# Both ends, the S5 tables and the start of attention of a hybrid S5 and attention block

## The chip, the cores and the metric

One core of a Trainium2 chip runs the whole block in one launch. The metric is the device time of one execution in microseconds (us). Each engine takes its own instructions in order: PE does matmuls, DVE, ACT and POOL work on tiles, SP issues most DMAs; ACT issues some from its own queue. Semaphores tie the queues together.

## The reference, cut to what matters

```python
h    = modulate(rmsnorm(x, norm1_g), sh1, sc1)            # x 1024x1024, one sequence; mod = silu(c) @ w_ada + b_ada
u, q, k, v, gate_a, gate_b = split(h @ w_in, ...)         # 512, 512, 512, 512, 1024, 1024 columns
# S5: 32 groups of 16 channels, 64 complex states; a linear recurrence over time
y    = gelu(Re(states @ C) + d_skip * u)
y    = y * sigmoid(y @ w_glu + b_glu)
y_a  = y @ w_a
# stick-breaking attention, 8 heads of 64, strictly causal, blocks of 128 queries
y_b  = stick_breaking_attention(q, k, v) @ w_b
x    = x + g1 * ((sigmoid(gate_a) * y_a + sigmoid(gate_b) * y_b) @ w_o)
h    = modulate(rmsnorm(x, norm2_g), sh2, sc2)
x    = x + g2 * ((silu(h @ w_ffn_gate) * (h @ w_ffn_up)) @ w_ffn_down)    # hidden width 2816
return rmsnorm(x, norm_f_g)
```

All is float32. A float32 product is made from three matmuls of rounded parts: each operand is split into a high part (a cast to fp32r) and a low part (the difference), and `PRODUCTS` runs high x high, high x low, low x high.

## The kernel before

The stages run one after the other, and PE's order is the order of the stages, with the matmuls of other stages put between where a scheduler finds room.

**Start (0 to 60 us).** x comes in tiles of 128 rows. ACT and DVE make sums of squares, PE transposes the tiles (L643, into `tp`), and the adaLN vectors are made meanwhile: `ada_products` (L989) multiplies `cond` with 512-column pieces of `w_ada`, which arrive as `pb`, and L621 sums over partitions into `adap`. L649 to L654 modulate, L660 projects u.

**S5 (90 to 265 us).** Four steps m of eight groups. DVE builds tables (`o`, L279 to L281, and `rt`, L291 to L296; DMAs L301 lay `rt` into `tz`, which POOL's memset L298 clears first), runs the scan (L327 to L342) and writes the states `h` (L345). PE adds `u x tz` (L354) and `h x o` (L355) in `s5a`, ACT copies that to `y` (L357), DMAs write it to `yD`. `o` and `tz` have one buffer each. In the same time PE runs the v projection (`v_proj`, L781) and the gates (`gate`, L760). Their results leave PSUM in turn on ACT and DVE: `vst` (L785), `gst` (L796 DVE, L798 ACT).

**GLU and y_a (254 to 359 us).** `glu` reads `yD` back (L1050) in eight pieces `raw`, L1051 does the gelu and writes with a stride of eight elements, `split` (L1038 ACT cast, L1039 DVE subtraction) makes `yp`, and L760 multiplies into `ga`. `branch_a` multiplies by the gate (L1087, into `na`).

**Attention (359 to 660 us).** `attention` goes through units (head pair, query block, key blocks). PE makes scores `z` (L834), DVE adds the causal mask where the block is on the diagonal (L896), ACT and DVE make log terms (L899 to L904), PE sums them with triangular ones (`acc<-wh,upto`), carried from unit to unit in `row` tiles, and multiplies by V. Between the parts of units `fillers` gives PE matmuls of the later q, k and gate projections (`JOBS`, in numbers `FILL`). The mask and the triangle `upto` are made at its start (POOL L822 to L830, DVE L825), and the carries are cleared there by DVE (L950).

**y_b and on (660 to 1456 us).** `branch_b` begins with the products of `w_b`; between its second and third column `ada_cols` turns the second half of the adaLN vectors into columns (L1030, single-column matmuls). Then come w_o, the FFN, and the last norm. Of the last row tile the sum of squares is taken in two halves (L1464), POOL makes small terms of the first (L1467) and multiplies its left half by `gf` (L1468); `rstd_p` (L510 to L514, ACT and POOL) makes the factor, L1439 and L1440 apply it, two DMAs write.

Of the kernel before, what the change touches and what calls it, by code (L numbers as in the profile page):

```python
# [28 lines left out]
class S5:  # L29
# [233 lines left out]
    def outputs(self, m):  # L263
# [5 lines left out]
        o = work.tile([128, 8, 9, 16], F32, name="o")  # L269
# [27 lines left out]
        tz = work.tile([128, 8, 128], F32, name="tz")  # L297
# [6 lines left out]
    def run(self, m, u_src, y_dst, more):  # L304
# [44 lines left out]
        for hf in range(2):  # L349
# [7 lines left out]
            nc.scalar.copy(y[:, 4 * hf:4 * hf + 4].rearrange("p g c -> p (g c)"), p)  # L357
# [21 lines left out]
FILL = (8, 8, 12)  # L379
JOBS = (("q", 1), ("k", 1), ("g", 0), ("g", 1), ("q", 2), ("k", 2), ("g", 2), ("q", 3), ("k", 3), ("g", 3), ("g", 4), ("g", 5), ("g", 6), ("g", 7))  # L380
# [49 lines left out]
class Block:  # L430
# [132 lines left out]
    def start(self, const, up, s5p):  # L563
# [8 lines left out]
        with self.pool("s0", 1, side="right") as sp, self.pool("s0a", 1, side="right") as ap, self.pool("s5t", 1, side="right") as st, \  # L572
# [66 lines left out]

            def turn(h, k):  # L640
                q = turned[h, k] = tp.tile([P, 512], F32, name="tp")
                for t in range(4):
                    nc.tensor.transpose(q[:, P * t:P * t + P], x[4 * h + t][:, P * k:P * k + P], self.ident)  # L643
# [23 lines left out]
            self.rows(const)  # L667
# [102 lines left out]
    def v_proj(self, vp):  # L770
# [3 lines left out]
        for c in range(2):  # L774
            ws = [self.w3(self.weight(src[:, 4 * a:4 * a + 4, 1536 + 256 * c:1792 + 256 * c], first=self.last_ada), 256) for a in range(2)]
            for t in range(KT):
# [8 lines left out]
                (nc.vector.tensor_copy if t % 2 else nc.scalar.copy)(v, ps[:, 0:256])  # L785
                nc.sync.dma_start(out=self.vD[P * t:P * t + P, 256 * c:256 * c + 256], in_=v)

    def gate(self, g, m, gp, first=None, ring=None, mm=None):
        nc = self.nc
        w = self.w3(self.weight(self.in_cols(2048 + 1024 * g + P * m), first=first, ring=ring, hi_eng=g and nc.gpsimd or None, lo_eng=g and nc.gpsimd or None))  # L790
        for h in range(2):
# [3 lines left out]
            if h:  # L795
                nc.vector.tensor_copy(st, ps)  # L796
            else:
                nc.scalar.copy(st, ps)  # L798
# [37 lines left out]
    def fillers(self, qk, qp, kp, gp):  # L836

        nc = self.nc
# [4 lines left out]
        def load(j):  # L843
            n, i = jobs[j]
            c0 = {"q": 512, "k": 1024, "g": 3072}[n] + P * i
            loaded.append(self.w3(self.weight(self.in_cols(c0), lo_eng=nc.gpsimd, hi_eng=nc.gpsimd if n == "g" else None, ring=rings[j % 3])))
# [28 lines left out]
    def scores(self, u, qk, work):  # L875
# [3 lines left out]
        q, k = qk[u.hp]  # L879
        u.a, s = (work.tile([P, 2, 512], F32, name=t, bufs=b) for t, b in (("wa", WAB2), ("ws", WSB)))  # L880
        u.parts = [work.tile([P, 2, 512], F32R, name=t, bufs=WHB) for t in ("wh", "wl")]
# [12 lines left out]
        if diag:  # L894
            m = P * (2 - len(u.kbs))
            nc.vector.tensor_tensor(a, z, self.mask[:, m:m + f].unsqueeze(1).broadcast_to([P, 2, f]), ALU.add)  # L896
# [45 lines left out]
    def attention(self, qk, qp, kp, vp, op, gp, work):  # L942
# [5 lines left out]
        for n in range(RWB):  # L948
            t = work.tile([P, 2, 512], F32R, name=f"row{n}")
            nc.vector.tensor_scalar(t.rearrange("p a (b c) -> p (a b) c", c=P), self.ident.unsqueeze(1).broadcast_to([P, 8, P]), 0.0, None, ALU.mult)  # L950
# [7 lines left out]
        fill = self.fillers(qk, qp, kp, gp)  # L958
# [6 lines left out]
        for i in range(-LOOK, len(units) + 1):  # L965
# [56 lines left out]
    def ada_cols(self, const, tp, pp):  # L1022

        nc = self.nc
        ps = pp.tile([P, 512], F32, name="pa")
        for a in range(2):
            t = tp.tile([P, 1024], F32, name="ac")
            nc.sync.dma_start(out=t.rearrange("p (a b) -> p a b", a=2), in_=self.aD[:, 2 + 2 * a:4 + 2 * a])
            for k in range(KT):
                nc.tensor.matmul(ps[:, 8 * a + k:8 * a + k + 1], lhsT=t[:, P * k:P * k + P], rhs=self.ones[:, 0:1], start=True, stop=True)  # L1030
# [577 lines left out]
```

## Time and profile before

| | us |
|---|---|
| three runs | 1449.16, 1455.71, 1457.14 (median 1455.71) |
| profiled execution, its time | 1457.32 |
| its span | 1455.6 |
| PE busy | 1408.4 (97%) |
| DVE, ACT, POOL busy | 1076.4, 640.4, 514.1 |
| mean granted TensorE clock | 0.986 |

PE is busy in all but 47.2 us of the span, so what counts is where PE waits, and where its clock is not granted in full. A view by windows shows both. An engine's busy time elsewhere matters only where PE waits for it. The ends of matmuls are modelled.

### The profile page before, as it was taken

How to read it: one execution, taken by the hardware profiler on the slowest of the kernel's cores; microseconds unless marked ns; L12 is line 12 of the kernel's file. 1: busy time of each engine (PE TensorE's matmuls, PEld its weight loads, DVE VectorE, ACT ScalarE, POOL GpSimd, SP SyncE). 2: the span in 40 equal slices, each digit the busy share in tenths (PEclk: the TensorE clock that was granted, in tenths of full speed). 3: DMA queues.
4: the chain of work that ended last, by engine and by line, in shares of the span. 5: the costliest groups of instructions: out<-in, count | busy, mean ns of one | idle time of the engine just before them, and what ended most of it. 6: DMA issues, size and time to landing. Idle time of an engine off the chain costs nothing. (4 is left out here: it accounts for less than half of the span.)

```text
span 1455.6 us, 18298 instructions
## 1 busy us (share of the span) xinstructions
PE 1408.4 (97%) x6730; PEld 1116.9 (77%) x6730; DVE 1076.4 (74%) x1395; ACT 640.4 (44%) x846; POOL 514.1 (35%) x291
## 2 busy tenths in 40 slices
PE   5999998999899999999999999999999999999997
PEld 3799887787666666658888888788888888788886
DVE  4779995456787889887723688777666667899896
ACT  3532112722586867674417543232323333433334
POOL 1010000102111022103400015876767566699394
PEclk9999999999999999999999999999999999999999
DMA  9665655489111112117452223644434369899722
GB/s 339 166 148 164 185 133 139 131 272 330 34 44 46 35 52 73 37 58 238 133 186 88 87 87 112 221 145 155 136 126 146 119 206 373 289 378 359 247 83 116
DMA packets 193561, 233.39 MB, mean 160 GB/s; under 512 B 29500, under 2 KB 128896, under 8 KB 193472
## 3 DMA queue, kind: packets, MB, share of 16 engines
q1 hardware_dynamic: 184336, 224.70, 47.1%
q10 hardware_dynamic: 8912, 7.48, 1.8%
q8 instruction: 53, 0.87, 0.2%
q14 instruction: 36, 0.29, 0.1%
q0 software_dynamic: 224, 0.05, 0.0%
HBM read 162.85 MB, written 68.16 MB: 159 GB/s over the span
## 5 line engine op out<-in xcount | busy, mean ns | idle before, releaser
L475 POOL TENSOR_TENSOR ws<-wb 128x1024 f32<-128x1024 f32 x24 | 60.7, 2527 | 175.8 <-DVE wl L478 148.1
L459 POOL TENSOR_TENSOR wl<-ws,wh 128x1024 fp32r<-128x1024 f32 x12 | 30.8, 2564 | 160.6 <-ACT wh L456 160.1
L927 DVE TENSOR_TENSOR wa<-wa,acc 128x512 f32<-128x512 f32 (+1 forms) x80 | 47.0, 628 | 32.9 <-ACT row L925 30.5
L1349 POOL TENSOR_TENSOR pa<-pa 128x512 f32<-128x512 f32 x30 | 63.4, 2143 | 0.3
L1293 POOL TENSOR_TENSOR f<-f,f 128x512 f32<-128x512 f32 x30 | 53.1, 1797 | 26.1 <-DVE f L1287 20.8
L899 ACT ACTIVATE ws<-wa 128x1024 f32<-128x1024 f32 (+1 forms) x40 | 39.1, 977 | 50.9 <-DVE wa L896 50.4
L904 DVE TENSOR_TENSOR wl<-ws,wh 128x1024 fp32r<-128x1024 f32 (+1 forms) x40 | 57.1, 1427 | 1.0
L478 DVE TENSOR_TENSOR wl<-ws,wh 128x1024 fp32r<-128x1024 f32 x23 | 41.4, 1798 | 20.2 <-ACT wh L477 20.1
L1004 DVE SCALAR_TENSOR_TENSOR acc<-aw,cond,acc 128x512 f32<-128x512 f32 x56 | 45.7, 816 | 10.2 <-DMA aw<-in_w_ada_dram 9.4
L456 ACT CAST wh<-ws 128x1024 fp32r<-128x1024 f32 x24 | 25.2, 1050 | 55.5 <-PE wo L1139 25.7
L902 DVE SCALAR_TENSOR_TENSOR ws<-wa,ws 128x1024 f32<-128x1024 f32 (+1 forms) x40 | 45.5, 1137 | 4.6 <-ACT ws L901 3.6
L834 PE MATMUL z<-q,k 64*128 64x512 f32 (+3 forms) x192 | 42.6, 534 | 6.1 <-DVE wa L896 4.9
L1378 POOL TENSOR_TENSOR pa<-pa,row 128x1024 f32<-128x1024 f32 x14 | 42.5, 3052 | 14.7 <-DMA pa<-in_w_ffn_down_dram 14.7
L1286 ACT ACTIVATE f<-f 128x1024 f32<-128x1024 f32 x20 | 21.2, 1061 | 59.5 <-DVE f L1324 30.8
L930 ACT ACTIVATE wa<-wa 128x1024 f32<-128x1024 f32 (+1 forms) x40 | 38.8, 971 | 19.3 <-DVE wa L927 18.3
L477 ACT CAST wh<-ws 128x1024 fp32r<-128x1024 f32 x23 | 24.1, 1054 | 50.9 <-PE wo L1302 15.6
L458 POOL TENSOR_SCALAR wh<-ws 128x1024 fp32r<-128x1024 f32 x6 | 7.5, 1245 | 105.0 <-issue 36.1
L477 ACT CAST wh<-wb 128x1024 fp32r<-128x1024 f32 x25 | 26.2, 1052 | 39.9 <-PE mm L1423 9.7
L475 POOL TENSOR_TENSOR wgs<-wb 128x1024 f32<-128x1024 f32 x12 | 28.9, 2405 | 40.8 <-DVE wl L478 19.9
L1423 PE MATMUL tq<-f,f 128*128 128x512 f32 x136 | 41.7, 389 | 0.0
L834 PE MATMUL mm<-wa,V 128*64 128x512 f32 (+3 forms) x192 | 39.8, 507 | 0.0
L478 DVE TENSOR_TENSOR wl<-wb,wh 128x1024 fp32r<-128x1024 f32 x25 | 38.1, 1528 | 1.9 <-ACT wh L477 1.9
(862 smaller groups left out, 4693.9 us busy)
## 6 DMA issues: line engine op xcount, KB each, us to landing
wb<-hD SPq DMA_DIRECT2D x40, 512.0 KB, 5.3
aw<-in_w_ada_dram SPq DMA_DIRECT2D x64, 256.0 KB, 4.3
hD<-f SPq DMA_DIRECT2D x30, 512.0 KB, 5.0
ws<-in_w_in_dram SPq DMA_DIRECT2D x23, 512.0 KB, 4.4
wb<-in_w_ffn_gate_dram SPq DMA_DIRECT2D x44, 256.0 KB, 4.2
wb<-in_w_ffn_up_dram SPq DMA_DIRECT2D x44, 256.0 KB, 4.6
ws<-hD SPq DMA_DIRECT2D x20, 512.0 KB, 4.8
x<-in_x_dram SPq DMA_DIRECT2D x16, 512.0 KB, 6.9
```

The source lines that it names most:

```text
L475: (add or nc.gpsimd).tensor_tensor(st, a, b, op)
L477: nc.scalar.copy(h, a)
L478: self.last_lo = (lo or nc.vector).tensor_tensor(l, a, h.bitcast(F32), ALU.subtract)
L834: return self.tc.keep_in_program_order(self.nc.tensor.matmul(*args, **kw))
L902: nc.vector.scalar_tensor_tensor(st, a, 0.0, st, ALU.max, ALU.add)
L904: nc.vector.tensor_tensor(lt, st, ht.bitcast(F32), ALU.subtract)
L927: nc.vector.tensor_tensor(a[:, x, 0:f], a[:, x, 0:f], r[:, x, 0:f], ALU.subtract)
L1004: nc.vector.scalar_tensor_tensor(acc, w[:, j], cj, acc, ALU.mult, ALU.add)
L1293: self.last_sum = nc.gpsimd.tensor_tensor(o, a, b, op)
L1349: self.after(nc.gpsimd.tensor_tensor(t[:, n], part(a), part(b), SIGN_B[i]), first)
L1378: self.after(nc.gpsimd.tensor_tensor(w, w, g2, ALU.mult), first)
L1423: nc.tensor.matmul(ps, lhsT=o[x][:, P * t:P * t + P], rhs=o[y][:, R], start=(j == 0), stop=(j == 3 * np_ - 1))
```

## The change

Five parts. (1) S5's tables `o` and `tz` get two buffers; the gelu is done by the copy of `s5a` out of PSUM (L357), so that `glu` loads y whole in four DMAs and reads it by stride in `split` and in the product with the sigmoid. (2) All `vst` copies are on ACT; the `gst` copies are on ACT, but for the gates that have `first` set, whose copies are all on DVE. (3) At the start PE transposes the identity 78 times before x is there, and 4 and 9 times round the first adaLN products. (4) The mask and triangles are made before `qk_proj`; `gt` and `na` have a pool of their own, with the result that attention's score tiles lie elsewhere; the carries are cleared after the first mask addition; `ada_cols` becomes four jobs "a" among the fillers; six fillers go into each of the last three units. (5) Of the last row tile, DVE instead of POOL multiplies by `gf`, and ACT makes the two small terms.

```diff
-        o = work.tile([128, 8, 9, 16], F32, name="o")
+        o = work.tile([128, 8, 9, 16], F32, name="o", bufs=2)
-        tz = work.tile([128, 8, 128], F32, name="tz")
+        tz = work.tile([128, 8, 128], F32, name="tz", bufs=2)
-            nc.scalar.copy(y[:, 4 * hf:4 * hf + 4].rearrange("p g c -> p (g c)"), p)
+            nc.scalar.activation(y[:, 4 * hf:4 * hf + 4].rearrange("p g c -> p (g c)"), p, AF.Gelu_apprx_tanh)
...
-FILL = (8, 8, 12)
-JOBS = (... ("g", 4), ("g", 5), ("g", 6), ("g", 7))
+FILL = (8, 8, 12, 6)
+JOBS = (... ("g", 4), ("a", 0), ("g", 5), ("a", 1), ("g", 6), ("a", 2), ("g", 7), ("a", 3))
...
+            def idle(n):
+                for _ in range(n):
+                    nc.tensor.transpose(acc[3][:, 0:P], self.ident, self.ident)
...
+            idle(78)
             for t in range(4):
                 square(t, t % 2 == 0)
...
+            idle(4)
             ada_sums(0)
+            idle(9)
...
-                (nc.vector.tensor_copy if t % 2 else nc.scalar.copy)(v, ps[:, 0:256])
+                nc.scalar.copy(v, ps[:, 0:256])
...
-            if h:
-                nc.vector.tensor_copy(st, ps)
-            else:
-                nc.scalar.copy(st, ps)
+            (nc.vector.tensor_copy if first else nc.scalar.copy)(st, ps)
...
+            if n == "a":
+                ps = self.mm.tile([P, 512], F32, name="mm")
+                for k in range(4):
+                    self.pinned(ps[:, k:k + 1], lhsT=loaded[j][:, P * k:P * k + P], rhs=self.ones[:, 0:1], start=True, stop=True)
+                    if k == 3:
+                        s = slice(4 * i, 4 * i + 4)
+                        nc.vector.tensor_tensor(self.mod2[:, s], ps[:, 0:4], self.cols[:, 88 + 4 * i:92 + 4 * i], ALU.add)
+                        ...
+                    yield
+                continue
...
-            t = work.tile([P, 2, 512], F32R, name=f"row{n}")
-            nc.vector.tensor_scalar(t.rearrange("p a (b c) -> p (a b) c", c=P), self.ident..., 0.0, None, ALU.mult)
+            t = rowp.tile([P, 2, 512], F32R, name=f"row{n}")
...
+                if i == -LOOK:
+                    for t in carries:
+                        self.after(nc.vector.tensor_scalar(t..., self.ident..., 0.0, None, ALU.mult), self.masked)
                 some(FILL[1] if i >= 0 else FILL[2])
+            elif i < len(units):
+                some(FILL[3])
...
-            yv = y[:, m].rearrange("p (c j) -> p j c", j=8)
-            for j in (0, 4):
-                raw = yp_.tile([P, 4, P], F32, name="raw", bufs=2)
-                nc.sync.dma_start(out=raw, in_=self.yD[P * m:P * m + P, j:j + 4])
-                nc.scalar.activation(yv[:, j:j + 4], raw, AF.Gelu_apprx_tanh)
+            nc.sync.dma_start(out=y[:, m].rearrange("p (j c) -> p j c", j=8), in_=self.yD[P * m:P * m + P])
         for m in range(4):
-            self.split(yp[:, 0, m], yp[:, 1, m], y[:, m])
+            self.split(*(yp[:, n, m].rearrange("p (c j) -> p c j", j=8) for n in range(2)), y[:, m].rearrange("p (j c) -> p c j", j=8))
...
-                    nc.vector.tensor_tensor(sg, y[:, m, s], sg, ALU.mult)
+                    yv, sv = y[:, m].rearrange("p (j c) -> p c j", j=8), sg.rearrange("p (c j) -> p c j", j=8)
+                    nc.vector.tensor_tensor(sv, yv[:, 64 * h:64 * h + 64], sv, ALU.mult)
...
-            if c == 2:
-                self.ada_cols(const, tp, pa)
...
             if t == ROWS[-1]:
+                nc.vector.tensor_tensor(row[:, L], row[:, L], gf[:, L], ALU.mult)
                 r = self.rstd_p(ss[:, 1:2], small[:, t, 2:3], small[:, t, 3:4], (small[:, t, 4:5], small[:, t, 5:6]))
...
-                            nc.gpsimd.tensor_scalar(small[:, t, n:n + 1], ss[:, 0:1], f / 1024.0, self.eps[:, n - 4:n - 3], ALU.mult, ALU.add)
-                        nc.gpsimd.tensor_tensor(row[:, cs], row[:, cs], gf[:, cs], ALU.mult)
+                            nc.scalar.activation(small[:, t, n:n + 1], ss[:, 0:1], AF.Identity, bias=self.eps[:, n - 4:n - 3], scale=f / 1024.0)
...
+                        self.triangles(s3.enter_context(self.pool("tri", 1)))
                         qk = [self.qk_proj(0, qp, kp, None)]
```

The rest of the diff moves tiles between pools (`rows`, `na`, `row`, `part`, `cp`), widens `eps` and lets `branch_b` begin at another PSUM bank.

How the rows stand on the engines, at three places. The line numbers of the changed kernel are its own: its L767 is L760 of before, L1030 is L1004, L1095 is L1087, L918 is L896, L1004 is L950.

PE at the last step of S5, before: the gate matmuls (`mx<-pa` or `pb` and a weight half) that stand ahead of the last y matmuls (`s5a`).

```order
L760 MATMUL mx<-pb,wl 128x512
L760 MATMUL mx<-pb,wh 128x512 x2
L760 MATMUL mx<-pb,wl 128x512
L354 MATMUL s5a<-u,tz 128x128
L355 MATMUL s5a<-h,o 128x128
```

The same place in the changed kernel:

```order
L767 MATMUL mx<-pa,wl 128x512
L767 MATMUL mx<-pa,wh 128x512 x2
L767 MATMUL mx<-pa,wl 128x512
L354 MATMUL s5a<-u,tz 128x128
L355 MATMUL s5a<-h,o 128x128
```

The last y matmuls have moved up before the second part (`pb`) of that gate; counted over the whole row, 30 gate matmuls that stood ahead of them stand behind them.

DVE at the last states `h` of S5, before (`scr`, `tc`, `tn` are the scan and its rotations; `gst` is a gate's copy):

```order
L345 TENSOR_TENSOR h<-scr 64x4x127 x2
L341 TENSOR_TENSOR scr<-scr,tc 128x4x127
L342 TENSOR_TENSOR scr<-scr,tn 128x4x127
L796 COPY gst<-mx 128x512
L345 TENSOR_TENSOR h<-scr 64x4x127 x2
L459 TENSOR_TENSOR wgl<-wgs,wgh 128x1024
```

And in the changed kernel:

```order
L345 TENSOR_TENSOR h<-scr 64x4x127 x2
L341 TENSOR_TENSOR scr<-scr,tc 128x4x127
L342 TENSOR_TENSOR scr<-scr,tn 128x4x127
L345 TENSOR_TENSOR h<-scr 64x4x127 x2
L459 TENSOR_TENSOR wgl<-wgs,wgh 128x1024
```

One of six `gst` copies (and all eight `vst` copies) that stood ahead of the last `h` is gone there; nothing else is added or taken away ahead of it.

DVE where attention begins, before (`na` is the product with the gate, `acc<-aw,cond,acc` an adaLN sum of a later stage, `row` the carries, `wa<-z,mask` the first masked scores):

```order
L1087 TENSOR_TENSOR na<-ga,gt 128x512
L1004 SCALAR_TENSOR_TENSOR acc<-aw,cond,acc 128x512
L950 TENSOR_SCALAR row_3531<-ident 128x1024
L950 TENSOR_SCALAR row_3533<-ident 128x1024
L825 CAST upto<-tri 128x128
L896 TENSOR_TENSOR wa<-z,mask 128x2x384 x2
```

And in the changed kernel:

```order
L1095 TENSOR_TENSOR na<-ga,gt 128x512 x2
L1030 SCALAR_TENSOR_TENSOR acc<-aw,cond,acc 128x512 x2
L918 TENSOR_TENSOR wa<-z,mask 128x2x384
L1004 TENSOR_SCALAR row_3617<-ident 128x1024
L1004 TENSOR_SCALAR row_3618<-ident 128x1024
L924 SCALAR_TENSOR_TENSOR ws<-wa,ws 128x2x384
L918 TENSOR_TENSOR wa<-z,mask 128x2x384
```

The first mask addition now stands ahead of the carries, the triangle's cast is gone from here (it stands some thirty rows earlier), and one adaLN sum more stands between the last `na` and the mask.

More of the change, by code (lines that the diff above doesn't have):

```diff
@@ L665, in store @@
                 nc.sync.dma_start(out=self.uD[P * m:P * m + P, :, 64 * h:64 * h + 64], in_=u)
-            self.rows(const)
+            self.rows(ap)
             load(0)
@@ L843, in load @@
         def load(j):
+            nonlocal turn
             n, i = jobs[j]
+            if n == "a":
+                t = cp.tile([P, 512], F32, name="ac", bufs=2)
+                nc.sync.dma_start(out=t, in_=self.aD[:, 2 + i])
+                loaded.append(t)
+                return
             c0 = {"q": 512, "k": 1024, "g": 3072}[n] + P * i
-            loaded.append(self.w3(self.weight(self.in_cols(c0), lo_eng=nc.gpsimd, hi_eng=nc.gpsimd if n == "g" else None, ring=rings[j % 3])))
+            loaded.append(self.w3(self.weight(self.in_cols(c0), lo_eng=nc.gpsimd, hi_eng=nc.gpsimd if n == "g" else None, ring=rings[turn % 3])))
+            turn += 1
         for j in range(AHEAD):
@@ L873, in fillers, with scores @@
                         yield
-    def scores(self, u, qk, work):
+    def scores(self, u, qk, part, work):
         nc = self.nc
         q, k = qk[u.hp]
+        u.parts = [part.tile([P, 2, 512], F32R, name=t) for t in ("wh", "wl")]
         u.a, s = (work.tile([P, 2, 512], F32, name=t, bufs=b) for t, b in (("wa", WAB2), ("ws", WSB)))
-        u.parts = [work.tile([P, 2, 512], F32R, name=t, bufs=WHB) for t in ("wh", "wl")]
         z = self.zp.tile([P, 2, 512], F32, name="z")
@@ L940, in values, with attention @@
             self.nc.scalar.copy(out[:, 512 * u.Q:512 * u.Q + 512], g.av)
-    def attention(self, qk, qp, kp, vp, op, gp, work):
+    def attention(self, qk, qp, kp, vp, op, gp, rowp, part, work, cp):
         nc = self.nc
@@ L957, in attention @@
                     units.append(Bag(hp=hp, Q=Q, kbs=kbs, group=g))
-        fill = self.fillers(qk, qp, kp, gp)
+        fill = self.fillers(qk, qp, kp, gp, cp)
         def some(n):
@@ L979, in attention @@
             if i + LOOK < len(units):
-                self.scores(units[i + LOOK], qk, work)
+                self.scores(units[i + LOOK], qk, part, work)
+                if i == -LOOK:
+                    for t in carries:
+                        self.after(nc.vector.tensor_scalar(t.rearrange("p a (b c) -> p (a b) c", c=P), self.ident.unsqueeze(1).broadcast_to([P, 8, P]), 0.0, None, ALU.mult), self.masked)
                 some(FILL[1] if i >= 0 else FILL[2])
+            elif i < len(units):
+                some(FILL[3])
         some(10000)
@@ L1020, in ada_row @@
             nc.vector.tensor_tensor(row[:, js], ps, row[:, js], ALU.add)
[L1022 to L1030, printed above, removed]
-        self.mod2 = const.tile([P, 16], F32, name="mod2")
-        self.G2 = const.tile([P, KT], F32, name="G2")
-        nc.vector.tensor_tensor(self.mod2, ps[:, 0:16], self.cols[:, 88:104], ALU.add)
-        nc.vector.scalar_tensor_tensor(self.G2, self.mod2[:, 8:16], 1.0, self.cols[:, 56:64], ALU.add, ALU.mult)
     def split(self, hi, lo, src, eng=None):
@@ L1144, in attend_out @@
         mod, G = self.mod2, self.G2
-        self.eps = const.tile([P, 19], F32, name="eps")
+        self.eps = const.tile([P, 27], F32, name="eps")
         for n, x in enumerate((1e-6, -0.5e-6, 1.5)):
@@ L1537, in run @@
                     op = s3.enter_context(self.pool("o", 4))
-                    with self.pool("tri", 1) as tri, self.pool("work", 1) as work, self.pool("zp", ZPB, PSUM) as self.zp, self.pool("acc", 1, PSUM) as self.accp, \
+                    with self.pool("row", 1) as rowp, self.pool("part", WHB) as part, self.pool("work", 1) as work, self.pool("zp", ZPB, PSUM) as self.zp, self.pool("acc", 1, PSUM) as self.accp, \
                             self.pool("mx", MXB, PSUM) as mx:
                         self.avp = mg_
-                        self.triangles(tri)
                         self.mm = Turns((mm, "mm"), *[(mx, "mx")] * MXB)
                         qk = [list(qk[0])] + [[None, None] for _ in range(3)]
-                        ops = self.attention(qk, qp, kp, vp, op, gp, work)
+                        with self.pool("cp", 1, side="right") as cp:
+                            ops = self.attention(qk, qp, kp, vp, op, gp, rowp, part, work, cp)
                         spare = []
```

25 lines of the change are left out of this document (15 added, 10 removed).

## Prediction

> **What bounds the kernel now.** I read the page first, then PE's waits, then the windows round each wait.
>
> ```profile
> PE 1408.4 (97%) x6730; PEld 1116.9 (77%) x6730; DVE 1076.4 (74%) x1395; ACT 640.4 (44%) x846; POOL 514.1 (35%) x291
> ```
>
> PE is the bound: 47.2 of 1455.6 us are left to it. In the waits (engine, line, what it waited for, total, times, longest) are the places:
>
> ```profile
> PE tp L643 <- ACT x L636: 13.7, 1, 13.7
> PE z L834 <- DVE wa L896: 4.9, 1, 4.9
> PE s5a L354 <- DMA gD<-gst: 4.9, 1, 4.9
> PE acc L834 <- DVE row L929: 3.7, 3, 1.3
> PE ga L760 <- ACT yp L1038: 2.3, 2, 1.9
> PE z L834 <- DVE na L1087: 1.2, 1, 1.2
> PE ga L760 <- DVE yp L1039: 0.8, 1, 0.8
> ```
>
> The first is the arrival of x, which the change doesn't touch. The others together are 17.8 us, and behind several of them stands a second cost, which the windows show (start:end, length, each engine's busy time, granted clock PEclk, DMA share, GB/s):
>
> ```profile
> 20.00:30.00 10.00, 7.67 (x50) 4.01 (x46) 6.52 (x24) 3.60 (x5) 0.00 (x0) 0.66 1.09 350
> 234.50:241.50 7.00, 4.24 (x20) 4.27 (x21) 0.79 (x2) 0.45 (x1) 0.00 (x0) 0.51 0.89 244
> 268.70:275.60 6.90, 6.30 (x14) 4.53 (x15) 1.94 (x3) 5.89 (x7) 0.00 (x0) 0.51 0.48 153
> 367.70:374.60 6.90, 5.81 (x14) 3.86 (x15) 4.39 (x5) 4.22 (x5) 0.04 (x1) 0.51 0.00 1
> 682.00:692.00 10.00, 10.00 (x47) 8.71 (x47) 9.96 (x9) 4.96 (x8) 6.45 (x4) 0.66 0.63 192
> ```
>
> Five times the clock falls to half. Each costs 3.4 us of full-clock work: 6.9 us at 0.51, or 10 us at 0.66, is 3.4 us short. Three follow waits of PE (S5's 4.9, GLU's 3.1, attention's 4.9). The fourth, at 682, has no wait in it (PE busy 10.00 of 10.00) but the single-column matmuls of `ada_cols`, and the first is in the start. So PE's waits and half-clock stretches that the change can reach are about 35 us.
>
> **The start.** The identity's last step, the first transposes, the adaLN products before and after the clock rose, the last weight's arrival:
>
> ```profile
> 2.25 0.31 POOL masks.py:199 TENSOR_SCALAR_AFFINE_SELECT ident<-ident 128x128 f32<-128x128 f32 x1
> 13.69 2.17 PE L643 MATMUL tp<-ident,x 128*128 128x128 f32 x8 [13.69 <-ACT x L636]
> L643 PE MATMUL tp<-ident,x x36: 271/273/474, 13.7 to 59.2; 128*128 128x128 f32 x36
> 16.78 3.27 PE L989 MATMUL mm<-pb,cond 128*32 128x256 f32 x32 [0.38 <-DVE cols L561]
> 46.72 1.93 PE L989 MATMUL mm<-pb,cond 128*32 128x256 f32 x32
> 45.41 1.05 ACT L596 CAST u3h<-ws 128x1024 fp32r<-128x1024 f32 x1 [0.23 <-DMA ws<-in_w_in_dram]
> ```
>
> The first 32 records took 3.27 us, the same 32 later 1.93: the start runs at half pace, though the clock column there reads 1.00. If 78 dummy transposes raise the clock, 1.34 us come off here and 3.4 with the stretch at 22.97. But the DMA engines are full (1.09), and the last weight's cast waits for its DMA at 45.4; ACT's squares and DVE's scales stand behind it. So the upper end is 4.7 us. The lower: the first eight transposes lie (2.17 - 0.47) / 7 = 0.24 apart, at full clock half that; 7 us at the one pace and the other 49 at 0.12 end at 2.6 + 7 + 5.9 = 15.5, which is 1.8 after x. I take +1.4, nearer the DMA's end. The two smaller `idle` groups lie in waits of PE.
>
> **S5.** What the last y matmuls wait for: DVE's last `h` (its end 233.9 + 1.4 = 235.3), and the tables in `tz`, which came as late.
>
> ```profile
> L785 DVE COPY vst<-mm 128x256 f32<-128x256 f32 x4 | 1.7, 414 | 0.9 <-DMA vD<-vst 0.9
> L796 DVE COPY gst<-mm 128x512 f32<-128x512 f32 x3 | 2.0, 683 | 0.0
> L785 DVEq EVENT_SEMAPHORE  x10: 21/35/2933, 105.9 to 141.6; - x10
> DVE o L280 <- PE s5a L355: 3.7, 1, 3.7
> DVE acc L1004 <- DMA aw<-in_w_ada_dram: 7.0, 7, 2.3
> ACT vst L785 <- DMA vD<-vst: 17.9, 4, 7.2
> 233.93 1.40 DVE L345 TENSOR_TENSOR h<-scr 64x508 f32<-64x508 f32 x2
> 224.67 0.62 PE L760 MATMUL mx<-pb,wh 128*128 128x512 f32 x2
> ...
> 226.71 0.61 PE L760 MATMUL mx<-pb,wh 128*128 128x512 f32 x2
> ```
>
> The rows of `vst` and `gst` show half of them (the others read another bank, `mx`). Ahead of the last `h` DVE loses eight `vst` copies (8 x 0.41 = 3.3 us) and six `gst` copies (6 x 0.68 = 4.1), 7.4 us, and a wait of 2.9 on a `vst` DMA that now falls to ACT: 10.3 us. PE comes earlier too, by the 30 gate matmuls that moved behind: nine (two, then one, alternating) take 226.71 - 224.67 = 2.04 us, so 30 take 6.8. The wait that is left is 4.9 + 6.8 - 10.3 = 1.4 us. If the 3.7 us that DVE waited for the single `o` come off as well, it is 0; if DVE gains nothing, it is 11.7. I take 1.4, too short to lower the clock: waits of 1.2 and 1.9 elsewhere did that only where others followed at once. Gain 4.9 - 1.4 + 3.4 = 6.9. `tz` in two buffers is cleared and filled behind the step before, so DVE's `h` should be last, not a DMA.
>
> The fourteen copies cost ACT 14 x 0.59 = 8.3 us at most (0.59 is L357's, below, of the larger shape); ACT is busy for 44% of the span. Behind a waiting `vst` copy on ACT stand the `inj` and `rt` copies of S5: that is a rival below.
>
> **GLU.** What ACT and DVE do to y, before:
>
> ```profile
> L357 ACT COPY y<-s5a x8: 586/586/589, 164.4 to 243.4; 128x512 f32<-128x512 f32 x8
> L1051 ACT ACTIVATE y<-raw x8: 1127/1150/1217, 258.5 to 273.4; 128x512 f32<-128x512 f32 x8
> L1038 ACT CAST yp<-y x4: 1044/1045/1052, 261.6 to 274.6; 128x1024 fp32r<-128x1024 f32 x4
> L1039 DVE TENSOR_TENSOR yp<-y,yp x4: 1224/1225/1226, 262.8 to 275.7; 128x1024 fp32r<-128x1024 f32 x4
> ```
>
> Eight gelus at 1.15 us (9.2 us) and a table load leave the path; in L357 they cost about what the copy costs, 0.59, under the scan. Between the last y matmul and the first `ga` PE now has 126 gate matmuls, 28.6 us, where it had 96. From the last copy of y (its end 243.4 + 0.6 = 244.0) to the first gelu (258.5) were 14.5 us of DMA and table load; to that come one cast and four subtractions, 1.05 + 4 x 1.23 = 6.0, together 20.5 of the 28.6. The strided reads have no price in the trace. The nearest row is L1051 against L357: by stride the same shape took 1.96 times as long. With that factor on casts and subtractions: 14.5 + 2.05 + 4 x 2.41 = 26.2, still hidden. So the 3.1 us of waits and the 3.4 behind them go: 6.5. If the factor were above 2.3, the rest would show as a wait.
>
> A rule that speaks against this: the Trainium skill, "SBUF — State Buffer", section "Door 1: The DMA port swizzle", says that each access to a new 16-byte line of SBUF is penalised, so that fp32 is free only up to a stride of four elements; the stride here is 128. L1051 agrees in kind (1.15 against 0.59 at a stride of eight, written). By the rule the sum is the 26.2 us just worked out, and the time the same.
>
> **Start of attention.**
>
> ```profile
> 359.87 2.80 DVE L1004 SCALAR_TENSOR_TENSOR acc<-aw,cond,acc 128x512 f32<-128x512 f32 x1
> 365.34 2.01 DVE L950 TENSOR_SCALAR row<-ident 128x1024 fp32r<-128x1024 f32 x2 [2.67 <-DMA aD<-acc]
> 367.78 0.96 DVE L896 TENSOR_TENSOR wa<-z,mask 128x768 f32<-128x768 f32 x1 [0.20 <-POOL mask L830]
> ```
>
> DVE stood 2.67 us for DMAs that read the memory the carries take, then 2.01 on the carries and for POOL's mask. Early mask, own pools and later carries put the mask addition right behind the last adaLN sum: the last `na` ends where L1004's row begins, near 359.9, two sums follow (2.80 us beside POOL's work, and another that I put at 0.8), then the addition of 0.96: its end is near 364.5, where it was 368.74. PE wants it 4.9 before that, at 363.9: 0.6 left, with about 0.8 for the first z and 1.0 for the third (the carries and one L924 now stand ahead of the second mask addition): 2.4 instead of 6.1, with no half clock behind. Gain 3.7 + 3.4 = 7.1; if the clock falls all the same, 3.7.
>
> **ada_cols and the end of attention.**
>
> ```profile
> 682.29 4.21 PE L1030 MATMUL wo<-ones,ac 128*128 128x1 f32 x32
> ```
>
> As fillers the 32 records cost about the same, 0.4 less at full clock. Spread in fours among wide matmuls they should not lower the clock: 3.8. Six fillers (each 0.23 us) in three units are 4.1 us of work beside the waits for `row` at 642 and 648 (1.3 and 1.2 of the 3.7); they were run behind them before. Gain 2.3, the third wait stays.
>
> **The last rows.**
>
> ```profile
> 1447.36 1.58 POOL L1467 TENSOR_SCALAR ss<-ss,eps 128x1 f32<-128x1 f32 x2
> 1448.91 1.25 POOL L1468 TENSOR_TENSOR pa<-pa,gf 128x512 f32<-128x512 f32 x1
> 1451.26 0.75 DVE L1440 SCALAR_TENSOR_TENSOR pa<-pa,ss,gf 128x512 f32<-128x512 f32 x1 [2.60 <-POOL ss L514]
> ```
>
> POOL's factor stood behind its own 1.58 + 1.25 us. Without them it follows the second square: two ACT terms (0.3 each, in front of that square) come in, then 1.5 us of L510 to L514. DVE's multiplication (0.68) fits in its 2.60 us of waiting. Bounds 0 and 2.8; I take 1.3.
>
> **Sum.** 1.4 + 6.9 + 6.5 + 7.1 + 3.8 + 2.3 + 1.3 = 29.3 us. The profiled execution took 1457.3 (span 1455.6 and 1.7 round it), so 1428.0; that execution is 1.6 above the median, 1455.7, and the three runs lie 8 us apart. I take 1428. Own range 1420 (S5's wait and attention's rest gone as well, start at 4.7) to 1435 (one stretch of half clock stays, strides show).
>
> **Rivals.**
> - *The warm-up does nothing* (20%). For it: the eight transposes at 13.69 ran at half pace to their end; against: PE had only just begun. Then 78 at 0.24 end at 2.6 + 18.7 = 21.3, 7.6 late, of which PE's waits behind them (20 to 30: busy 7.67 of 10) give back some; I take 6 lost and 1.4 not gained: 1435. The Trainium skill, "TensorE: Matmul & The Clock Gate", Part 4, says that transposes don't count as PE's being busy; no run here shows it yet.
> - *S5's wait only moves* (10%). DVE stood 7.0 us in S5 for adaLN weights; if its chain comes no earlier, PE, 6.8 us early, waits 11.7 at a lower clock. S5 then loses 6.8 where 6.9 were gained: 1428 + 13.7 = 1442.
> - *Half clock stays* (9%): the short waits that remain (1.4, 2.4) and the "a" jobs still meet the gate. Without three to four of the 3.4: 1428 + 12 = 1440.
> - *Slower: ACT's queue holds S5 up* (6%). Four waits of ACT's own `vst` copies for their DMAs took 17.9 us, 4.5 each. If the eight moved copies waited so, with S5's `inj` behind them, S5 came 36 us later: 1457.3 - 29.3 + 36 + 3.4, near 1467. From 26 us on it is slower than before. Against: most of those waits lay where ACT had nothing else.
>
> **Chances.** The forecast has 55%; with the warm-up rival, 75% lie in 1420 to 1436. The range reaches to 1442 for the two middle rivals, and to 1417 below. A difference of 0.5% (7.3 us) is about what can be told from none: faster 0.89, same 0.06, slower 0.05.
>
> **What would show it.** Right: no wait above 2 us in PE's waits but the first; PEclk 1.00 at 235, 269, 368 and 685; L989's first group under 2.2 us; `ga` without a wait; first mask addition done within 6 us of the last `ga`. Wrong: s5a L354 waiting for `h` or `tz` over 4 us, ACT's `vst` waits growing into `inj`, strided casts above 2.4 us.

## The result, and the profile after

The changed kernel takes 1434.36 us (median of 4 runs, 1432.96 to 1436.13) against 1453.45 before (4 runs, 1449.16 to 1457.14): ratio 0.9873, 95% interval 0.9846 to 0.9901. The gain is 19 us (14 to 22 by the interval) where 27.7 were forecast. The two profiled executions are 1436.13 and 1457.32, 21.2 apart, and the terms below are measured between these two. Waits of PE after (engine, line, what it waited for, total, times, longest):

```profile
PE mm L642 <- POOL ident masks.py:199: 2.6, 1, 2.6
PE z L838 <- DVE na L1095: 2.6, 1, 2.6
PE mm L664 <- ACT pa L653: 2.4, 2, 2.2
PE z L838 <- DVE wa L918: 1.8, 2, 1.2
PE mm L664 <- DVE pa L658: 1.7, 2, 0.8
PE wo L1429 <- DVE f L478: 1.3, 1, 1.3
PE acc L838 <- DVE row L951: 1.2, 1, 1.2
```

The waits for `tz` (4.9), for `yp` (3.1) and the long one for the mask (4.9) are gone. Two have grown: L664 for `pa` in the start (1.3 and 1.0 before, now 2.4 and 1.7) and the first z for `na` (1.2, now 2.6). By windows (start:end, length, busy PE, PEld, DVE, ACT, POOL, PEclk, DMA share, GB/s):

```profile
20.00:30.00 10.00, 8.94 (x76) 6.48 (x76) 6.86 (x26) 3.63 (x6) 0.00 (x0) 1.00 1.09 350
51.90:54.10 2.20, 0.02 (x1) 0.02 (x1) 0.93 (x7) 1.04 (x3) 0.00 (x0) 1.00 1.04 343
54.80:61.60 6.80, 5.96 (x16) 4.59 (x16) 3.36 (x6) 1.60 (x2) 0.00 (x0) 0.50 0.01 2
224.00:230.00 6.00, 6.00 (x37) 5.29 (x36) 1.75 (x3) 0.59 (x1) 0.00 (x0) 1.00 0.83 237
347.30:355.00 7.70, 3.95 (x21) 2.70 (x20) 6.82 (x8) 2.96 (x3) 2.73 (x1) 1.00 0.58 211
680.00:690.00 10.00, 10.00 (x46) 8.29 (x45) 9.24 (x10) 3.60 (x6) 6.13 (x4) 1.00 0.57 188
```

Four of the five half-clock stretches are gone from this profile (S5, GLU, attention, `ada_cols`). The first has moved, from 23 us to 54.8, behind the new wait in the start. Attention's is not gone for good: in five of the eight other profiles with the same order there (x1_no_idle, x2_sums_first, x8_cols_back, x10_one_buffer, x11_dve_copies) 3.4 us at half clock still stand between 346 and 358 us.

When PE comes to the same matmul in both profiled executions gives the terms as measured:

| stretch | forecast gain | measured |
|---|---|---|
| to the first v projection (84.73, after 87.39) | 1.4 | -2.65 |
| on to the last `ga<-y2p` (S5 and GLU) | 6.9 + 6.5 | 14.1 |
| on to attention's first `acc` | 7.1 | 4.2 |
| on to the end of w_b's products | 3.8 + 2.3 | 5.05 |
| on to PE's last matmul (w_o, FFN) | 0 | -0.5 |
| the last rows | 1.3 | 1.0 |

### The profile page after: what moved, and what is told of

Its sections match the earlier page's. It is cut to its first block, busy times and chain, and to the rows that moved or that the text cites. A ratio compares the mean times of both kernels' runs of the same rounds, so it can differ in the third digit from the quotient of the medians.

```text
span 1434.4 us, 18472 instructions
## 1 busy us (share of the span) xinstructions
PE 1408.1 (98%) x6821; PEld 1121.3 (78%) x6821; DVE 1078.4 (75%) x1388; ACT 639.9 (45%) x852; POOL 514.5 (36%) x288
## 4 chain that ended last, share of the span: by engine, by line
PE 80%; DVE 9%; DMA 5%; ACT 3%; issue 2%; POOL 1%; SPq 0%; ACTq 0%; POOLq 0%; DVEq 0%
PE tq L1308 12%; PE wo L1308 6%; PE tq L1429 6%; PE mm L1308 6%; PE mx L838 5%; PE mm L838 5%; PE mm L767 4%; PE mm L1429 3%; PE mx L767 3%; PE wo L1429 3%; PE acc L838 2%; PE wo L1145 2%; PE mm L1145 2%; PE mm L664 2%; PE z L838 2%
## 5 line engine op out<-in xcount | busy, mean ns | idle before, releaser
L1030 DVE SCALAR_TENSOR_TENSOR acc<-aw,cond,acc 128x512 f32<-128x512 f32 x56 | 45.7, 817 | 9.1 <-DMA aw<-in_w_ada_dram 8.4
L1292 ACT ACTIVATE f<-f 128x1024 f32<-128x1024 f32 x20 | 21.2, 1061 | 60.6 <-DVE f L1330 31.4
L475 POOL TENSOR_TENSOR wgs<-wb 128x1024 f32<-128x1024 f32 x12 | 28.9, 2407 | 41.4 <-DVE wl L478 20.3
```

Source lines behind the costliest of these rows:

```text
L475: (add or nc.gpsimd).tensor_tensor(st, a, b, op)
```

## The experiments

| run | median us (lowest to highest) | ratio to before, 95% interval |
|---|---|---|
| the change | 1434.36 (1432.96 to 1436.13) | 0.9873, 0.9846 to 0.9901 |
| x1_no_idle | 1432.53 (1430.52 to 1435.75) | 0.9849, 0.9822 to 0.9875 |
| x2_sums_first | 1430.6 (1429.35 to 1430.98) | 0.9831, 0.9806 to 0.9857 |
| x3_s5_only | 1447.6 (1444.83 to 1450.8) | 0.995, 0.993 to 0.997 |
| x4_rest_early | 1432.8 (1431.1 to 1435.9) | 0.9854, 0.9828 to 0.9881 |
| x5_eps19 | 1442.32 (1441.46 to 1444.95) | 0.9922, 0.9904 to 0.994 |
| x6_s5_pad | 1437.36 (1436.28 to 1440.74) | 0.9888, 0.9869 to 0.9907 |
| x7_three_edits | 1427.63 (1427.04 to 1429.63) | 0.982, 0.98 to 0.9839 |
| x8_cols_back | 1441.4 (1437.95 to 1444.74) | 0.9911, 0.9892 to 0.9931 |
| x9_cols_bank | 1432.12 (1430.96 to 1434.48) | 0.9841, 0.9816 to 0.9865 |
| x10_one_buffer | 1440.74 (1438.79 to 1442.5) | 0.9896, 0.9874 to 0.9918 |
| x11_dve_copies | 1433.54 (1433.44 to 1436.0) | 0.9851, 0.9827 to 0.9875 |
| x12_gelu_in_glu | 1432.63 (1430.32 to 1433.71) | 0.984, 0.9816 to 0.9864 |

Differences of 2 us between rows of this table are not told apart by it. Each ratio is to runs of the kernel before taken beside that row, whose medians go from 1452.98 to 1456.88; so where two times and their ratios disagree, the difference is that uncertain.

### The start

```diff
# x1_no_idle, against the changed kernel
-            idle(78)
-            idle(4)
-            idle(9)
```

> The changed kernel without its 91 dummy transposes. Theory: the end of the start is set by the last u weight, whose DMA lands at 45.4 us, and by the chain on DVE and ACT behind it (the last part of the modulated x at 53.3 us in both profiles), so the warm-up only turned 3.7 us of earlier matmuls into a wait of 3.0 us and a half-clock stretch at 54.8. Then this one is 2 to 3.5 us faster than the changed kernel (v projection begins near 84.7 us, not 87.4), near 1431. Rival, as forecast: the warm-up gains 1.4 us or more, and this one is 1 to 5 us slower.

Measured: 1432.53, 1.8 under the change; the v projection begins at 85.2. The direction is the theory's, the size not safely apart from nothing; the rival, a gain of the warm-up, is not seen. Why, the changed kernel's own rows show (PE, ACT and DVE in the start):

```profile
2.62 10.86 PE L642 MATMUL mm<-ident 128*128 128x128 f32 x78 [2.62 <-POOL ident masks.py:199]
16.68 1.93 PE L1015 MATMUL mm<-pb,cond 128*32 128x256 f32 x32 [0.38 <-DVE cols L561]
45.37 1.05 ACT L596 CAST u3h<-ws 128x1024 fp32r<-128x1024 f32 x1 [3.87 <-DMA ws<-in_w_in_dram]
51.46 0.16 DVE L485 TENSOR_SCALAR rv<-ss 128x4 f32<-128x4 f32 x1
53.25 0.78 ACT L653 ACTIVATE pa<-tp,mod,G 128x512 fp32r<-128x512 f32 x1 [1.16 <-DVE G L625]
54.08 0.50 PE L664 MATMUL mm<-pa,u3h 128*128 128x512 f32 x1 [2.19 <-ACT pa L653]
```

The 78 transposes take 10.86 us and the first adaLN products 1.93 (3.27 before): here the warm-up does what it is for. But the last weight is cast at 45.37 as before (45.41) and `pa` comes at 53.25 (53.38). What PE wins turns into a wait, and after it the clock falls. It doesn't last in every execution, either: in three of the eight profiles with this start (x5_eps19, x9_cols_bank, x10_one_buffer) the clock fell again at 15.6 to 16.5 us, for 3.4 to 10.2 us, and the first products ran at half pace. Those three have no half clock at 55 and begin the v projection at 84.2 to 84.6; the five whose clock held begin it at 85.6 to 87.4.

```diff
# x2_sums_first, against the changed kernel
                     square(7, True)
-                    next(steps)
-                    r = self.rstd(const, ss[:, 4:8], 4)
                 ada_sums(g + 1)
+                if g == 2:
+                    r = self.rstd(const, ss[:, 4:8], 4)
...
             for t in range(4, 8):
                 scale(r, t)
+            next(steps)
             s5.load()
```

> The changed kernel with the last adaLN sums ahead of the second half's norm factor, and 2.7 us of S5's small DVE operations behind the modulation instead of ahead of it. Theory: what PE waits for at 51.9 is the DVE queue (the norm factor behind the small operations, the modulation behind the factor), not the weight (its parts are ready at 47.7); then the modulated x comes near 51, the wait of 2.2 shrinks below 1, the half-clock stretch at 54.8 is gone, and it is 4 to 6 us faster than the changed kernel. Rival: the weight or x holds PE, the wait stays, and the time is the same within 1 us.

Measured: 1430.6, 3.8 faster than the change, a little under the theory's 4 to 6, and every run below the change's lowest (the intervals of the two ratios overlap). The same two rows of this run (DVE, ACT):

```profile
50.01 0.17 DVE L485 TENSOR_SCALAR rv<-ss 128x4 f32<-128x4 f32 x1 [0.76 <-ACT sqa L630]
50.56 0.76 ACT L653 ACTIVATE pa<-tp,mod,G 128x512 fp32r<-128x512 f32 x1
```

`pa` comes at 50.56, the wait of 2.2 is gone (the two of 0.8 for L658 stay), no half clock follows. So what held the end of the start was DVE's order behind the weight's DMA, not the DMA alone. The v projection begins at 82.5, 2.3 before the kernel before.

### S5 and GLU

```diff
# x3_s5_only, against the kernel before
-        o = work.tile([128, 8, 9, 16], F32, name="o")
+        o = work.tile([128, 8, 9, 16], F32, name="o", bufs=2)
... tz, vst and gst copies, gelu in L357 and y by stride as in the change
-            self.rows(const)
+            self.rows(ap)
# x6_s5_pad: x3_s5_only, and
-        self.eps = const.tile([P, 19], F32, name="eps")
+        self.eps = const.tile([P, 27], F32, name="eps")
# x5_eps19, against the changed kernel
-        self.eps = const.tile([P, 27], F32, name="eps")
+        self.eps = const.tile([P, 19], F32, name="eps")
```

> The kernel before with the S5 part alone (two buffers for o and tz, copies on ACT, gelu in the copy, y by stride; the adaLN rows' pool moved for room). Theory: the waits at S5's last step (4.9) and at GLU (3.1) and both half-clock stretches go: 13 to 15 us faster than before. Rival: it needs the other parts, because PE then comes earlier and DVE does not: 4.9 turns into a wait of up to 11.7 there, 0 to 8 us faster.

> The changed kernel with eps 19 columns wide again instead of 27: 32 bytes less in the pool that lies below the weights and operands, so those tiles begin at a multiple of 64 bytes, where in both kernels they begin 32 bytes past one. Theory, from the S5-only run, whose matmuls in the FFN stood 230 to 231 ns apart instead of 227 with those tiles so shifted: the pace of PE hangs on where its operands lie; the FFN stages take 6 to 9 us more, the whole 7 to 12 us slower than the changed kernel, near 1443. Rival: that spacing came from something else in the S5-only run, and the time here is the same within 1 us.

> The S5-only kernel with eps widened to 27 columns, nothing else: operands 32 bytes past a multiple of 64 again. Theory of the pace: matmuls back at 227 ns, and what the S5 part gave up to the end of attention (15.9 us by the S5-only profile) shows in the time: 6 to 9 us faster than the S5-only run, 11 to 15 faster than before. Rival: the S5 part is worth only the 5.4 us that the S5-only run showed, and this is the same as that run within 1 us.

Measured: x3_s5_only gains 5.4 us. That is far under the theory's 13 to 15, and in the rival's 0 to 8 but not by the rival's way: its profile has no wait for `s5a` and no half clock in S5 or GLU. It is 15.9 ahead of before at the end of attention, then loses 5.2 in 380 us of the FFN's L1302, at full clock and with less waiting than before (0.4 us against 1.1). Matmuls in the same 300 us of the FFN, before, x3_s5_only, x5_eps19 and the change in this order (start:end, length, PE busy and count, PEclk, DMA share, GB/s):

```profile
910.00:1210.00 300.00, 298.94 (x1319) 1.00 0.49 163
```

```profile
910.00:1210.00 300.00, 300.00 (x1306) 1.00 0.50 166
```

```profile
910.00:1210.00 300.00, 300.00 (x1306) 1.00 0.51 171
```

```profile
910.00:1210.00 300.00, 300.00 (x1325) 1.00 0.52 175
```

300 / 1306 = 229.7 ns for one, against 300 / 1325 = 226.4. `rows` left the lowest pool, and with it the tiles above that pool (weights, `pa`, `pb`) moved; eight more columns of `eps` move them by 32 bytes. By the addresses of the built programs, which no profile shows, the tiles go from 32 bytes past a multiple of 64 to the multiple itself, and the wider `eps` brings them back. With the old `eps` the changed kernel is 8.0 us slower (intervals apart), as expected; with the wide one the S5 part alone gains 16.7 instead of 5.4, a little more than expected (intervals apart). So the width of `eps`, which the prediction didn't look at, is worth 8 to 10 us in this kernel, only because another edit had moved the tiles.

```diff
# x10_one_buffer, against the changed kernel
-        o = work.tile([128, 8, 9, 16], F32, name="o", bufs=2)
+        o = work.tile([128, 8, 9, 16], F32, name="o")
... tz likewise
# x11_dve_copies, against the changed kernel
-                nc.scalar.copy(v, ps[:, 0:256])
+                (nc.vector.tensor_copy if t % 2 else nc.scalar.copy)(v, ps[:, 0:256])
... gst as in the kernel before (DVE where h is 1)
# x12_gelu_in_glu, against the changed kernel: L357 a copy, raw, L1051's gelu and contiguous reads back
```

> The changed kernel with one buffer each for o and tz again. As forecast the two buffers are the smaller part: DVE's last states come 3.7 us later (229.5 instead of 225.8), and the order puts the 30 gate matmuls back ahead of the last y matmuls, so PE comes 6.8 us later and doesn't wait: the same within 1.5 us. Rival: the two buffers are what takes the 4.9 us wait away; then a wait of 3 to 5 us and half clock behind it, 4 to 8 us slower.

> The changed kernel with half of the vst and gst copies on DVE again. As forecast these copies and the wait in them are the 10.3 us of DVE ahead of the last states: those come near 235, PE near 233, a wait of 2 to 4 us and half clock behind it: 3 to 7 us slower. Rival: the buffers alone do it, no wait: the same within 1.5 us.

> The changed kernel with the gelu back in glu (eight pieces raw, gelu written by stride, contiguous reads after). As forecast the longer cover (126 gate matmuls, 28.6 us) and the shorter chain together take GLU's wait away. With the old chain: 14.5 us of DMA, then 18.4 from the first gelu to the last subtraction, 32.9 against 28.6: a wait of 1 to 4 us and half clock behind it, 2 to 7 us slower. Rival: the cover alone does it, since PE needs the last part of y last; the same within 1.5 us, or faster by the cheaper reads.

Measured: one buffer 6.4 us slower (its lowest run above the change's highest); the copies back on DVE the same (0.8 faster); gelu back in glu the same (1.7 faster). By the ratios one buffer would cost 3.3, with intervals that overlap; but the next two rows of the table, taken beside it, lie 7.2 and 8.1 us lower, and no run of theirs reaches its lowest. All three theories, made from the forecast's working, missed, and the times are those of the rivals. A wait of each, in this order: DVE in x10_one_buffer, PE in x10_one_buffer, PE in x11_dve_copies.

```profile
DVE o L280 <- PE s5a L355: 4.5, 1, 4.5
```

```profile
PE mm L767 <- ACT wgh L456: 3.4, 1, 3.4
```

```profile
PE s5a L355 <- DVE h L345: 1.4, 1, 1.4
```

With one buffer DVE waits 4.5 us for `o` again and the order again has 96 gate matmuls, not 126, behind the last y; PE waits 0.9 for `tz`, then runs into the next weight's cast (3.4), and the clock is at half for 3.4 us behind it. With the copies on DVE the states come later, but the wait of 1.4 is for the third step's, at 212 us, and PE has none at the last step: the order has 104 gate matmuls behind the last y there, so 22 of the 30 have moved back ahead of it.

The profiles say how much each is worth in place, from the first v projection to the last `ga<-y2p`: 259.6 us in the change, 266.6 with one buffer, 262.45 with the copies back (1.7 of the 2.9 more are waits of PE), 259.6 with the gelu back. The profiled execution of x11_dve_copies (1436.0 us) is as long as the change's (1436.13) all the same, because in it the start took 1.8 us less, attention's start 0.3 and the FFN 0.9.

### Attention's start, ada_cols

```diff
# x4_rest_early, against the changed kernel
-            for n in ((8, 9), (10,), (11,), ())[c]:
+            for n in ((8, 9), (10, 11), (), ())[c]:
# x7_three_edits: x2_sums_first, x4_rest_early, and in ada_rest
-        acc = ap.tile([P, 512], F32, name="acc")
+        acc = ap.tile([P, 512], F32, name="acc", bufs=1 + (n > 7))
```

> The changed kernel with the last adaLN sum (n = 11) started one weight earlier in branch_a. Theory: the last two na wait behind three adaLN sums on DVE that came late because DVE had waited 3.5 us for their weights; without them the wait of z for na goes from 2.6 to about 1, the mask addition comes 2 us earlier, 1.5 to 3 us faster than the changed kernel. Rival: the sums are late because the DMAs are, wherever they stand; then another wait of the same length stands there or earlier and the time is the same within 1 us.

> The changed kernel with the adaLN sums of the start first (3.8 us faster by its run), the last adaLN sum of branch_a begun a weight earlier (1.6 us faster by its run), and two buffers for that stage's sum, since DVE waited 3.0 us there for the DMA that reads the one buffer out. Theory: they add, with 0.5 to 1.5 for the third: 6 to 7 us faster than the changed kernel, near 1428; the wait of z for na below 1 us. Rival: the two gains are the same half-clock stretch counted twice, or only noise: 4 us faster.

DVE where attention begins, in the changed kernel:

```profile
343.82 0.49 DVE L1028 TENSOR_SCALAR acc<-aw,cond 128x512 f32<-128x512 f32 x1 [3.50 <-DMA nD<-na]
346.40 2.32 DVE L1030 SCALAR_TENSOR_TENSOR acc<-aw,cond,acc 128x512 f32<-128x512 f32 x3
348.63 1.28 DVE L1095 TENSOR_TENSOR na<-ga,gt 128x512 f32<-128x512 f32 x2
354.04 0.94 DVE L918 TENSOR_TENSOR wa<-z,mask 128x768 f32<-128x768 f32 x1
```

The last two `na` stand behind adaLN sums that came late, because DVE had waited 3.5 us; PE's last `ga` ends at 347.4, `na` at 349.9. x4_rest_early is 1.6 faster (within the noise), its wait for `na` 1.8, where about 1 was expected. All three edits together: 1427.63, 6.7 us faster than the change, as expected, intervals apart, and the fastest kernel of all. Of that 3.8 are the first edit's by its own run; the 3.0 beyond are not told apart from nothing (the ratios' intervals of x2_sums_first and x7_three_edits overlap). Its waits of PE, and its clock:

```profile
PE mm L664 <- DVE pa L658: 1.6, 2, 0.8
PE wo L1430 <- DVE f L478: 1.3, 1, 1.3
PE acc L839 <- DVE row L952: 1.2, 1, 1.2
PE tq L1146 <- DVE wb L459: 1.1, 1, 1.1
PE z L839 <- DVE na L1096: 0.8, 1, 0.8
```

```profile
core 0: 1425.3 us, clock 0.998
```

There is no half-clock stretch in it after the first microseconds and before the last matmul. From the last `ga` to the first `acc` it takes 12.4 us (the change 16.1, before 20.3). But two profiles whose sums stand as in the change, x5_eps19 and x9_cols_bank, take 12.4 there too, with the same wait of 0.8 for `na`; so it is not shown that moving the sums brought it.

```diff
# x8_cols_back, against the changed kernel: ada_cols in branch_b again, no "a" jobs
-JOBS = (... ("a", 0), ("g", 5), ("a", 1), ("g", 6), ("a", 2), ("g", 7), ("a", 3))
+JOBS = (... ("g", 5), ("g", 6), ("g", 7))
+            if c == 2:
+                self.ada_cols(const, tp, pa)
# x9_cols_bank: x8_cols_back, and
-                    self.banks.n = 2
+                    self.banks.n = 1
```

> The changed kernel with ada_cols back in branch_b (32 single-column records in one piece) instead of the four jobs. Theory: as forecast, a half-clock stretch follows them near 665 us, 3 to 4 us slower than the changed kernel. Rival: the stretch came from where the clock's windows fell, and the jobs cost as much as the piece: the same within 1 us.

> The run before with ada_cols back in branch_b, but with branch_b's banks begun at 1 instead of 2, so that ada_cols' own bank brings them to the changed kernel's order from its third column on. Theory: the 6.2 us wait at w_o's start and the half clock behind it came from the bank order, not from ada_cols; without them only the half-clock stretch behind the single-column records stays: 1.5 to 4 us slower than the changed kernel. Rival: the piece itself costs the 7 us, and this is the same as that run within 1 us.

x8_cols_back is 7.0 slower, where 3 to 4 were expected. The stretch of half clock that was expected is there (3.4 us, at 666.6), and besides it a wait of PE with 10.2 us of half clock behind it:

```profile
PE tq L1162 <- DVE gb L1143: 6.2, 1, 6.2
```

`ada_cols` takes a PSUM bank, and with it in the order w_o's first output falls on the bank that is read out last. x9_cols_bank moves the bank: the wait is gone, and the time is 1432.12, 2.2 under the change, where 1.5 to 4 above it were expected. Its profile has a half-clock stretch of 6.8 us at 661, and from the first `acc` to the end of w_b's products it is 3.2 us slower than the change, as forecast. It wins that back elsewhere: 2.9 us in the start and 3.7 from the last `ga` to the first `acc` (12.4 us), and 1.0 each in w_o and the FFN. From the last `ga` to the first `acc` nine profiles with the change's order there took between 12.4 and 16.1 us, so this varies from execution to execution. The 1.0 in w_o does not: w_o takes 92.0 us with `ada_cols` in `branch_b` and no wait (before, x6_s5_pad, x9_cols_bank), and 93.0 to 93.7 with the jobs, where PE waits 0.7 to 1.4 for `wb` at its start (x3_s5_only and x5_eps19, with their slower matmuls, take longer). So the four jobs' gain is partly given back there, and it is not seen in the time. That the single-column piece lowers the clock is seen, though: all five profiles that have it in one piece show half clock behind it (3.4 or 6.8 us), and none of the nine that have it in four jobs does.

## Why the prediction was right, and where its working was not

**Sign, range and size.** 1434.4 lies in 1417 to 1442, at the upper edge of the forecast's own 1420 to 1435; the gain is two thirds of the forecast's. The reading that carried it, that PE's waits and the half clock that follows them are what there is to win, held: four of the five stretches, 3.4 us each, and the waits for `tz`, `yp` and the mask are gone from the profile. Three of the five signs named for being right came (the clock at full in four places, the first products under 2.2 us, `ga` without a wait); two did not: waits of 2.6 and 2.2 us are left, and the first mask addition is done 7.6 us behind the last `ga`, not 6.

**Where luck helped.** w_o and the FFN were put at 0, and -0.5 came. But the change moves `rows` out of the lowest pool, and without the wider `eps` that alone would have cost 8 us: the forecast gave no reason for its 0. And 1435, the time of the warm-up rival, is all but the measured one, though by that rival the transposes would have ended at 21.3 us at half pace; they ended at 13.5.

**The start was mis-sized**: 1.4 forecast, -2.65 in the profiled execution. Bounds of -1.8 and 4.7 were given, and it fell below both, since the sum counted the old half-clock stretch as gone and no new one. The text named the DMA's end at 45.4 and the chain behind it as the limit, and then didn't follow that a PE that comes 3.7 us early at such a limit must wait, and that a wait there lowers the clock. The eight profiles with the same start begin the v projection between 84.2 and 87.4, the four without the warm-up between 84.7 and 85.2: it won 0.5 at best, and lost where the clock held. What was left out besides is DVE's order: x2_sums_first, which changes only that, begins it at 82.5.

**The warm-up rival fell.** Transposes of the identity alone raised the clock; the change in two windows of the start (columns as above; PEclk reads 1.00 in both, but the trace's first record of the clock, which says full, comes at 7.0 us):

```profile
3.00:6.00 3.00, 3.00 (x16) 3.00 (x15) 0.11 (x1) 1.61 (x2) 2.56 (x6) 1.00 0.92 344
9.00:12.00 3.00, 3.00 (x30) 3.00 (x28) 1.73 (x5) 0.73 (x4) 0.00 (x0) 1.00 1.07 359
```

16 in 3 us, then 30: they stand 213 ns apart up to 7.0 us and 109 behind it. In x7_three_edits the first record comes at 7.5 and in x5_eps19 at 5.4, and the pace changes there. The Trainium skill, "TensorE: Matmul & The Clock Gate", Part 4, has it that the full clock doesn't engage for transposes, which don't count as PE's being busy in the same way. Here they brought it, and the measurement decides.

**S5 and GLU: right sum, wrong cause.** 13.4 forecast, 14.1 between the profiles, 16.7 by the S5 part alone. But the sum of S5 was built on fourteen copies leaving DVE (10.3 us), with the buffers as an extra of up to 3.7. The runs show the reverse: the buffers are worth 6.4 us by the time and 7.0 by the profile, the copies 2.9 by the profile and nothing by the time. The step that failed is the reading of what the last y matmuls waited for. Three rows of the kernel before:

```profile
220.03 1.43 DVE L280 TENSOR_TENSOR o<-C,A 128x576 f32<-128x576 f32 x2 [3.71 <-PE s5a L355]
227.26 1.92 PE L289 MATMUL s5a<-o,bst 128*16 128x128 f32 x16
237.26 0.77 PE L354 MATMUL s5a<-u,tz 128*128 128x128 f32 x2 [4.91 <-DMA gD<-gst]
```

DVE waits 3.71 us for the one `o`, until PE has done the y matmuls of the step before. Thirteen of the fourteen copies stand ahead of that wait (the last of them at 215.6), so without them it would only have been longer: PE was busy all the while and set its end. From `o` PE makes what becomes `rt` (L289), and the DMAs that lay `rt` into `tz` are issued up to 233.2 and land 2.5 to 4.7 us later. PE's wait, which is for `tz`, ends at 237.26; DVE's last `h`, which the forecast took for the limit, was done at 235.3. So what held PE was the chain from the single buffer, and the subtraction 4.9 + 6.8 - 10.3 took off copies that were not on it. (2.9 of the 10.3 was not lost by DVE at all: it is the length of a semaphore's record, and DVE stood idle for 0.9 there.) The same subtraction took the moved gate matmuls as given, while the order moves them back when DVE is later. In GLU the gelu's move was costed as needed beside the longer cover; the cover alone does it (x12_gelu_in_glu). The price of strides was right for the cast and too high for the subtraction:

```profile
L1049 ACT CAST yp<-y x4: 2034/2054/2065, 242.9 to 248.8; 128x1024 fp32r<-128x1024 f32 x4
L1050 DVE TENSOR_TENSOR yp<-y,yp x4: 2018/2028/2033, 245.0 to 251.4; 128x1024 fp32r<-128x1024 f32 x4
```

The cast went from 1.05 to 2.05 (1.96 times, the factor taken from L1051), the subtraction from 1.23 to 2.03 (1.65 times), and the last was done at 253.4, before `ga` began at 260.2. The rule of the Trainium skill's "SBUF — State Buffer" (section "Door 1: The DMA port swizzle") on lines of 16 bytes agrees in kind.

**Attention's start**: 7.1 forecast, 4.2 measured. The step that failed put the last `na` at 0.8 us behind the last `ga`; it was 2.6, since one adaLN sum more stood there and all came late. The two S5-only profiles, without any of these edits, take 16.6 and, with the wide `eps`, 15.4 from the last `ga` to the first `acc`; nine profiles with them take 12.4 to 16.1, the change itself 16.1. So as much comes without these edits, and what they win is not told apart from what varies there.

**ada_cols and fillers**: 6.1 forecast, 5.05 measured, of which w_o gives some 1.0 back; the waits at 642 and 648 went from 1.3 and 1.2 to 0.5 in all. **The end**: 1.3 forecast, 1.0. POOL's first small term took 0.97 beside DVE's multiplication, and the final product began 4.1 us behind PE's last matmul, where it was 5.2.

```profile
1428.13 0.97 POOL L512 TENSOR_SCALAR ss<-ss 128x1 f32<-128x1 f32 x1 [1.00 <-ACT ss L1474]
1429.95 0.75 DVE L1447 SCALAR_TENSOR_TENSOR pa<-pa,ss,gf 128x512 f32<-128x512 f32 x1 [0.89 <-POOL ss L514]
```

**Left open**: whether x7_three_edits with the gelu and the copies where they were would be faster still (the two were only taken back singly), why the next weight is late with one buffer, and what in the execution sets the 12.4 or 16 us at attention's start.

## What to carry to other kernels

Where PE comes earlier at a place that a transfer or another engine's queue fixes, the gain turns into a wait, and a wait of two microseconds can cost three more of half clock: look for what stands ahead of the late operand in its engine's order before speeding up PE. Before taking work off an engine, look for a wait of that engine between the work and the late operand: what stands ahead of such a wait is absorbed by it. When several edits are made for one wait, take each back alone: here two buffers were worth 6 to 7 us, the copies 3 at most and the gelu's move nothing. And after any change of what lies in the lowest pool, compare the spacing of matmuls in a stage that wasn't touched.

## What the runs showed of the hardware

- The pace of 512-column matmuls depends on where their operands begin: 226.4 ns apart, or 229.7 with 32 bytes less in a tile of the pool below them, and the kernel is 8.0 us longer. Which of the operands matters was not tried.
- Transposes alone bring the clock up: 213 ns apart, then 109 from the trace's first record of the clock on (7.0 us in the change).
- Thirty-two single-column matmuls in one piece are followed by half clock (3.4 us in three profiles, 6.8 in two) though PE has no wait there; in fours among wide matmuls they were not (nine profiles).
- The half clock comes in stretches of 3.4, 6.8 and 10.2 us, and the same waits don't always bring the same one: after the same two waits in the start (2.2 and 0.8) it took 6.8 us in one profile (the change) and 3.4 in four others (x4_rest_early, x8_cols_back, x11_dve_copies, x12_gelu_in_glu). Where the first wait was 1.8 or 1.9 (x10_one_buffer, x9_cols_bank) there was none; in those the clock had fallen at 16 us already, and PE came later.
